# Expert weights in 1 MB loads: two adjacent rows to a partition, in a decoder with two mixture-of-experts layers on one Trainium2 core

## The chip, the core and the metric

The kernel runs on one core of one Trainium2 chip. The time is the device time of one execution in microseconds; three executions of the kernel before took 2774.13, 2776.43 and 2777.44 us.

## What is computed

One sequence of 1024 tokens, 1024 features wide, in float32, passes two layers. The first mixes tokens with a gated DeltaNet, the second with differential attention; each mixer is followed by a layer norm and a hierarchical mixture of experts:

```python
group_prob = softmax(x @ w_group)                 # 4 groups, the best one is taken
in_group = (x @ w_expert) of that group           # 8 experts in it, the best two are taken
hcat = x_rows @ w13[e]                            # [rows, 1024] @ [1024, 1024]
hid = silu(hcat[:, :512]) * hcat[:, 512:]
y_rows = hid @ w2[e]                              # [rows, 512] @ [512, 1024]
h = layer_norm(ALPHA * h + sum of the two gated y_rows)
```

There are 32 experts in a layer, with 6 MB of float32 weights each (w13 4 MB, w2 2 MB), so 192 MB are read per layer.

## The kernel before

The order of the work is: the DeltaNet (`phase_a`), its output projection with the routing logits, `routing` (sorts the tokens by expert, largest expert first, and writes the index tables xidx and yidx), `experts`, `combine` (gates, residual, layer norm), attention (`phase_b_attention`), its output projection, and again `routing`, `experts` and `combine`.

**Experts.** `plan` (L1500) writes out the order of the work: experts in the order of `ORDER`, which mixes large ones with small ones. The numbers of rows that an expert is built for stand in `CAPS`; they are cut into blocks of at most 128 rows. In the first layer all experts have one block, 16 of them of 64 rows or less. In the second layer sizes are uneven: some experts have two or three blocks, and many have 16 to 64 rows. An expert has 12 pieces of weights, 128 rows of 1024 floats each (512 KB): 8 of w13 (the contraction over the features) and 4 of w2 (the contraction over hid). For each piece PE multiplies the block's transposed X or hid with it. The order of use is that of `seq` (L1530): pieces 0 to 4 of an expert's w13, then the 4 pieces of w2 of the expert before it, then pieces 5 to 7.

A block of more than 64 rows works with split weights: `cut_one` (L1426) has ACT cast a piece to `mh` and DVE compute the rest `ml`, and `mm3` multiplies three times. A block of at most 64 rows ("whole") multiplies the piece `mraw` itself, in float32, with two halves of PE's columns side by side. Casts are issued up to `AHEAD` = 9 pieces before the use (`use`, L1474), into a pool of `NHI` = 6 pairs. PE, ACT and DVE each work in the order in which this code issues (`InOrder`, L202).

**The ring of weights.** `Weights` (L1375) loads the pieces one by one from SyncE's queue (`load_one`, L1415) into a ring of slots of 512 KB: in the first layer 13 slots that exist while the output projection runs (5 in the pool m_kept, 8 in m_raw), and 9 more (m_late) once its memory is free; in the second layer 11 and 9. `load` (L1439) issues a load as soon as the code has passed the point where the slot's old piece is done: for a piece that only large blocks use that is its cast, otherwise PE's last use (`held`, L1391). The 12 pieces of the first expert go into the pool of mh and ml (`load_first`, L1433). The experts 1 and 2 are known before the routing (`FIXED`), and the ring is filled with them as far as it goes (`load_fixed`, L1451); later experts' numbers are read from `eid`.

**Gathers and transposes.** A block's rows of h are gathered by POOL with an indirect DMA into one of four X buffers (L1581), issued two experts ahead (`gather`, L1701). `trx` (L1607) transposes X with PE, 128 columns at a time, `trh` (L1646) does so with hid; the matrix to be transposed is PE's stationary operand, so a transpose has a weight load of that data and a matmul with the identity. Results are scattered to y in DRAM by POOL (L1671).

**Combine.** `combine` (L1785) loads y, two rows per token, 1 MB at a time (`yin`, L1802: rows 2p and 2p+1 of 256 to partition p), adds it to h and normalizes. h, and ln_ffn_g and ln_ffn_b, use slots of the weights' pools (`tile` and `spare`); in the first layer so do the first weights of the attention (`start`, L946).

Names in the profile: `mraw` is a weight piece in the ring (in combine also h, g or b), `mh` and `ml` the split piece, `xT`/`hT` and `xTw`/`hTw` the transposed operands of large and whole blocks, `mtr` and `mtw` the PSUM tiles of transposes, `acc` the products, `in_w` the weights in DRAM. L210 is the helper of `InOrder`, so all instructions of PE, ACT and DVE in the experts have this line; L1423 is the weight load.

Of the kernel before, what the change touches and what calls it, by code (L numbers as in the profile page):

```python
# [19 lines left out]
P = 128  # L20
# [22 lines left out]
NRAW, NKEPT, NLATE, NHI, AHEAD = (13, 11), 5, 9, 6, 9  # L43
# [110 lines left out]
def moe_setup(c, es):  # L154

    nc = c.nc
    p = es.enter_context(c.tc.tile_pool(reuse_waits="tile", name="moe", bufs=1, side="right"))
    consts(c, "moe", p)
    c.cb = p.tile([P, 2 * P + 3], BF16, name="cb")
    nc.vector.tensor_copy(c.cb[:, 0:P], c.tris)  # L160
    nc.vector.tensor_copy(c.cb[:, P:2 * P], c.ones)
    nc.vector.tensor_copy(c.cb[:, 2 * P:2 * P + 2], c.colv)
    nc.vector.memset(c.cb[:, 2 * P + 2:], 2.0 * T / P)
    c.tris_b, c.ones_b, c.colv_b, c.none_b = (c.cb[:, a:b] for a, b in ((0, P), (P, 2 * P), (2 * P, 2 * P + 2), (2 * P + 2, 2 * P + 3)))
    c.lg8 = p.tile([P, NT, 8], F32, name="lg8")
# [3 lines left out]
    c.xidx = p.tile([P, 256], I32, name="xidx")  # L169
    c.yidx = p.tile([P, 256], I32, name="yidx")  # L170
    c.ovl = p.tile([1, 2, NCOL + 1], I32, name="ovl")
    c.eid = p.tile([1, NE], I32, name="eid")
# [1201 lines left out]

class Weights:  # L1375
# [5 lines left out]
    def __init__(self, c, layer, kept, raw, seq):  # L1381
        self.late = None
        self.nearly = NRAW[layer]
        self.c, self.seq = c, seq
        self.w13, self.w2 = c.ins["w13"][layer], c.ins["w2"][layer]
        self.kept, self.raw, self.nraw = kept, raw, NRAW[layer] + NLATE
        self.first = [p for p, (r, _) in enumerate(seq) if r == seq[0][0]]
        self.ring = [p for p, (r, _) in enumerate(seq) if r != seq[0][0]]
        self.loaded = self.split = self.free = self.spares = 0
# [6 lines left out]
        self.extra = NKEPT - 2 - (3 if layer == 0 else 0)  # L1396
        self.tiles, self.ids = {}, {}
# [8 lines left out]
    def tile(self):  # L1406

        return self.kept.tile([P, D], F32, name="mraw")

    def spare(self):  # L1410

        self.spares += 1
        return self.tile() if self.spares <= self.extra else self.raw.tile([P, D], F32, name="mraw")

    def load_one(self, eid, i, raw=None):  # L1415
        if raw is None:
            n = self.loaded % self.nraw
            raw = self.tile() if n < NKEPT else (self.raw if n < self.nearly else self.late).tile([P, D], F32, name="mraw")
        if i < KT:
            src = self.w13[bass.ds(eid, 1), i * P:(i + 1) * P]  # L1420
        else:
            src = self.w2[bass.ds(eid, 1), (i - KT) * P:(i - KT + 1) * P]
        self.c.nc.sync.dma_start(raw, src.rearrange("a p f -> (a p) f"))  # L1423
        return raw
# [14 lines left out]
    def load(self, upto):  # L1439
        while self.loaded < min(upto, len(self.ring)):  # L1440
            if self.late is None and self.loaded >= self.nearly:
                return
            if self.loaded >= self.nraw:
                before = self.ring[self.loaded - self.nraw]
                if before >= (self.free if self.held[before] else self.split):
                    return
            r, i = self.seq[self.ring[self.loaded]]
            self.tiles[r, i] = (self.load_one(self.expert(r), i),)
            self.loaded += 1

    def load_fixed(self):  # L1451
        n = 0
        while n < len(self.ring) and self.seq[self.ring[n]][0] < FIXED:
            n += 1
# [84 lines left out]
def weights_open(c, layer, es):  # L1539

    moe_setup(c, es)
    kept = es.enter_context(c.tc.tile_pool(reuse_waits="tile", name="m_kept", bufs=NKEPT, side="right"))
    c.raw2 = ExitStack()
    raw = c.raw2.enter_context(c.tc.tile_pool(reuse_waits="tile", name="m_raw", bufs=NRAW[layer] - NKEPT, side="right"))
    c.jobs, c.steps, seq = plan(layer)
    c.w = Weights(c, layer, kept, raw, seq)


def experts_open(c, es):
# [3 lines left out]
    for x in c.X:  # L1553
        c.nc.gpsimd.memset(x, 0.0)
    c.w.hi = es.enter_context(tc.tile_pool(reuse_waits="tile", name="m_hi", bufs=NHI))
    c.w.late = es.enter_context(tc.tile_pool(reuse_waits="tile", name="m_late", bufs=NLATE))
# [4 lines left out]
def experts(c, layer, h_dram, y_dram):  # L1561
# [4 lines left out]
    with ExitStack() as es:  # L1566
# [22 lines left out]
        def turn(b, src, n, dst):  # L1589
# [3 lines left out]
            for i in range(n):  # L1593
                pe.transpose(pt[:, i, 0:R], src[0:R, i * P:(i + 1) * P], c.ident[0:R, 0:R])
# [4 lines left out]
        def plain(b, src, n, dst):  # L1599
# [3 lines left out]
            for i in range(n):  # L1603
                pe.transpose(pt[:, i, 0:R], src[0:R, i * P:(i + 1) * P], c.ident[0:R, 0:R])
# [140 lines left out]
        c.h = [w.spare() for t in range(HA[layer][1])]  # L1745
# [39 lines left out]
def combine(c, layer, h_dram, y_dram, dst, hT=None):  # L1785

    nc, tc, ins = c.nc, c.tc, c.ins
    with ExitStack() as es:
# [4 lines left out]
        c.h += [c.w.spare() for t in range(HA[layer][1], NT)]  # L1793
# [129 lines left out]
```

## Time and profile before

| | |
|---|---|
| median of three executions | 2776.43 us |
| the profiled execution | 2769.66 us, its span 2767.9 us |
| PE busy in the span | 2420.6 us (87%) |
| DVE, ACT, POOL | 1504.0, 1216.1, 550.2 us |
| moved by DMA | 564.01 MB, mean 204 GB/s; read from HBM 515.58 MB |
| weight loads of the ring | 720 of 512 KB, on SyncE's queue (q1) |
| mean granted PE clock | 0.946 |

The profile is one execution. Its page gives each engine's busy time, the span in 40 slices with the share of busy DMA engines and the rate, the waits with the instruction that ended each, and the DMA queues. Queue q1 is SyncE's, q0 holds POOL's gathers and scatters, q10 is ACT's. A DMA share is the mean over 16 engines of the time that packets took; packets in flight overlap, so it can pass 1. Busy PE is modelled from pipelined matmuls and is not PE at its peak.

### The profile page before, as it was taken

Reading aid. Unit: us, or ns where it says so; the run is one execution under the profiler, and the core shown is the slowest. Engines: PE = TensorE matmul, PEld = TensorE weight load, DVE = VectorE, ACT = ScalarE, POOL = GpSimd, SP = SyncE. Lnnn points to the kernel's source line nnn. Section 1 sums busy time; section 2 is a strip of 40 time slices with the busy share of each in tenths; the row PEclk is TensorE's granted clock in tenths of the full one; section 3 lists DMA queues with packets and bytes.
Section 4 is the critical chain, followed back from the end, with each engine's and each line's share of the span. In section 5 each row is a group of like instructions: output and inputs, shape, how many; then the busy total and the mean of one; then the engine's idle time right before and its main releaser. Section 6 shows DMA issues by size and latency. Waiting matters only on the chain. (4 is left out here: it accounts for less than half of the span.)

```text
span 2767.9 us, 38789 instructions
## 1 busy us (share of the span) xinstructions
PE 2420.6 (87%) x13789; PEld 1646.7 (59%) x13789; DVE 1504.0 (54%) x2696; ACT 1216.1 (44%) x2173; POOL 550.2 (20%) x445
## 2 busy tenths in 40 slices
PE   8999999999969998888559999998987897989990
PEld 5777777777735544444257777776764462545550
DVE  4555555564547554555376766676446432233467
ACT  5455555543425444444245555555332322122454
POOL 3333333331202111010132111111021111011104
PEclk9999999999989999999769999999997998999995
DMA  4121111124779999999831111012537969699885
GB/s 144 50 58 50 58 55 58 47 83 131 249 247 366 391 387 382 382 379 397 336 132 44 33 39 33 31 30 97 198 113 251 404 242 392 242 401 367 309 317 225
DMA packets 195480, 564.01 MB, mean 204 GB/s; under 512 B 40401, under 2 KB 63185, under 8 KB 193233
## 3 DMA queue, kind: packets, MB, share of 16 engines
q1 hardware_dynamic: 178240, 515.07, 50.7%
q0 software_dynamic: 15168, 43.01, 4.5%
q10 hardware_dynamic: 1872, 3.40, 0.4%
q8 instruction: 110, 1.80, 0.3%
q14 instruction: 90, 0.73, 0.1%
HBM read 515.58 MB, written 52.89 MB: 205 GB/s over the span
## 5 line engine op out<-in xcount | busy, mean ns | idle before, releaser
L210 DVE TENSOR_TENSOR ml<-mraw,mh 128x1024 fp32r<-128x1024 f32 x300 | 357.1, 1222 | 269.3 <-ACT mh L210 248.6
L210 ACT CAST mh<-mraw 128x1024 fp32r<-128x1024 f32 x300 | 307.2, 1052 | 272.7 <-DMA mraw<-in_w 205.4
L210 PE MATMUL acc<-mh,xT 128*128 128x512 f32 (+5 forms) x976 | 329.2, 406 | 3.2 <-ACT mh L210 3.2
L210 PE MATMUL acc<-mraw,xTw 128*64 128x512 f32 x1184 | 286.1, 615 | 13.6 <-DVE xTw L210 13.1
L185 POOL TENSOR_TENSOR wl<-raw,wh 128x512 fp32r<-128x512 f32 x106 | 155.1, 1484 | 485.7 <-ACT wh L184 421.4
L210 PEld LDWEIGHTS acc<-mh,xT 128*128 128x128 f32 (+5 forms) x976 | 166.5, 171 | 91.5 <-issue 24.6
L223 PE MATMUL pj<-xh,wh 128*128 128x512 f32 x512 | 217.9, 426 | 0.0
L224 PE MATMUL pj<-xl,wh 128*128 128x512 f32 x512 | 209.3, 409 | 0.0
L1581 POOL DMA_INDIRECT X<-h,xidx x69 | 71.4, 1035 | 689.3 <-PE mtw L210 374.9
L225 PE MATMUL pj<-xh,wl 128*128 128x512 f32 x512 | 207.7, 406 | 0.1
L210 PE MATMUL acc<-ml,xT 128*128 128x512 f32 (+5 forms) x496 | 195.9, 399 | 1.7 <-DVE ml L210 1.7
L223 PE MATMUL pj<-hT,wh 128*128 128x512 f32 (+1 forms) x432 | 165.8, 384 | 8.9 <-DVE kll L1010 5.4
L224 PE MATMUL pj<-hT,wh 128*128 128x512 f32 (+1 forms) x432 | 168.1, 389 | 0.0
L210 PEld LDWEIGHTS acc<-mraw,xTw 128*64 128x64 f32 x1184 | 76.2, 138 | 148.1 <-issue 108.9
L225 PE MATMUL pj<-hT,wl 128*128 128x512 f32 (+1 forms) x432 | 162.3, 376 | 1.7 <-POOL wl L185 1.6
L210 PE MATMUL acc<-mraw,hTw 128*64 128x512 f32 x592 | 143.5, 627 | 19.9 <-ACT hTw L210 19.4
L210 PE MATMUL acc<-mh,hT 128*128 128x512 f32 (+5 forms) x480 | 159.5, 403 | 0.6 <-ACT hT L210 0.5
L408 DVE SCALAR_TENSOR_TENSOR cv<-pr,cw,cv 128x512 f32<-128x512 f32 x144 | 118.9, 826 | 50.9 <-ACT cv L405 48.8
L1114 ACT ACTIVATE e<-sc,sm 128x256 f32<-128x256 f32 (+7 forms) x128 | 94.6, 742 | 89.8 <-DVE sm L1112 89.4
L210 PEld LDWEIGHTS acc<-mh,hT 128*128 128x128 f32 (+5 forms) x480 | 83.0, 173 | 49.7 <-issue 16.2
L225 PEld LDWEIGHTS pj<-xh,wl 128*128 128x128 f32 x512 | 97.2, 190 | 19.9 <-POOL wl L185 0.7
L224 PEld LDWEIGHTS pj<-xl,wh 128*128 128x128 f32 x512 | 97.5, 190 | 18.2 <-issue 1.7
(407 smaller groups left out, 4918.8 us busy)
## 6 DMA issues: line engine op xcount, KB each, us to landing
mraw<-in_w SPq DMA_DIRECT2D x720, 512.0 KB
raw<-in_w_in SPq DMA_DIRECT2D x32, 512.0 KB
yin<-y SPq DMA_DIRECT2D x16, 1024.0 KB
raw<-in_w_kvq SPq DMA_DIRECT2D x21, 512.0 KB
h<-res SPq DMA_DIRECT2D x16, 512.0 KB
p<-ores POOLq DMA_DIRECT2D x12, 512.0 KB, 3.8
res<-p SPq DMA_DIRECT2D x12, 512.0 KB
mh<-in_w SPq DMA_DIRECT2D x12, 512.0 KB
```

Source lines behind the costliest of these rows:

```text
L185: c.nc.gpsimd.tensor_tensor(l[:, s], src[:, s], h[:, s].bitcast(F32), OP.subtract)
L210: out = getattr(self.engine, name)(*args, **kwargs)
L223: mm(out, ah, bh, start=first, stop=False)
L224: mm(out, ah, bl, start=False, stop=False)
L225: mm(out, al, bh, start=False, stop=last)
L408: nc.vector.scalar_tensor_tensor(a, pr[:, 1 + j:513 + j], cw[:, idx, j:j + 1], a, op0=OP.mult, op1=OP.add)
L1114: nc.scalar.activation(e[:, 0:L], st[m][:, 0:L], AF.Exp, bias=sm[:, 2 + m:3 + m], scale=SC, accum_out=sm[:, 4 + m:5 + m])
L1581: c.last_gather = instruction(nc.gpsimd.indirect_dma_start(out=b.X[0:rows], out_offset=None, in_=h_dram, in_offset=bass.IndirectOffsetOnAx ...
```

## The change

A slot of the ring becomes 1 MB, two pieces. One DMA loads 256 rows of w13 or w2: rows 2p and 2p+1 go to partition p, side by side, so each partition gets 8 KB that are contiguous in DRAM. Piece i of a pair now holds rows i%2, i%2+2, ... of the 256, and the transposes of X and hid take every other column to match (`rows_of`). The ring has 7 + 4 slots of 1 MB in the first layer in place of 13 + 9 of 512 KB, and 5 + 5 in place of 11 + 9 in the second. A slot is reused when both of its pieces are done. The pool m_kept is gone; other users take half a slot each, from m_raw. The first expert's pieces are still loaded one by one (128 rows with a row step of two). The index tables are allocated later, beside the X buffers.

```diff
-NRAW, NKEPT, NLATE, NHI, AHEAD = (13, 11), 5, 9, 6, 9
+NRAW, NLATE, NHI, AHEAD = (7, 5), (4, 5), 6, 9
...
+def rows_of(i):
+    return slice(2 * P * (i // 2) + i % 2, 2 * P * (i // 2) + 2 * P, 2)
...
-        self.kept, self.raw, self.nraw = kept, raw, NRAW[layer] + NLATE
+        self.raw, self.nraw = raw, NRAW[layer] + NLATE[layer]
...
-        self.ring = [p for p, (r, _) in enumerate(seq) if r != seq[0][0]]
+        self.ring = [(r, i // 2) for r, i in seq if r != seq[0][0] and i % 2 == 0]
+        self.at = {key: p for p, key in enumerate(seq)}
...
     def tile(self):
-        return self.kept.tile([P, D], F32, name="mraw")
-    def spare(self):
-        self.spares += 1
-        return self.tile() if self.spares <= self.extra else self.raw.tile([P, D], F32, name="mraw")
+        if self.spare is None:
+            t = self.raw.tile([P, 2, D], F32, name="mraw")
+            self.spare = t[:, 1]
+            return t[:, 0]
+        t, self.spare = self.spare, None
+        return t
...
+    def load_one(self, eid, i, raw):
+        w, i = (self.w13, i) if i < KT else (self.w2, i - KT)
+        self.c.nc.sync.dma_start(raw, w[bass.ds(eid, 1), rows_of(i)].rearrange("a p f -> (a p) f"))
         return raw
+    def load_two(self, eid, u, raw):
+        w, u = (self.w13, u) if u < KT // 2 else (self.w2, u - KT // 2)
+        src = w[bass.ds(eid, 1), 2 * P * u:2 * P * (u + 1)]
+        self.c.nc.sync.dma_start(raw, src.rearrange("e (p a) f -> (e p) a f", a=2))
...
             if self.loaded >= self.nraw:
-                before = self.ring[self.loaded - self.nraw]
+                r, u = self.ring[self.loaded - self.nraw]
+                before = self.at[r, 2 * u + 1]
                 if before >= (self.free if self.held[before] else self.split):
                     return
-            r, i = self.seq[self.ring[self.loaded]]
-            self.tiles[r, i] = (self.load_one(self.expert(r), i),)
+            r, u = self.ring[self.loaded]
+            raw = (self.raw if self.loaded % self.nraw < self.nearly else self.late).tile([P, 2, D], F32, name="mraw")
+            self.load_two(self.expert(r), u, raw)
+            for a in range(2):
+                self.tiles[r, 2 * u + a] = (raw[:, a],)
             self.loaded += 1
...
-                pe.transpose(pt[:, i, 0:R], src[0:R, i * P:(i + 1) * P], c.ident[0:R, 0:R])
+                pe.transpose(pt[:, i, 0:R], src[0:R, rows_of(i)], c.ident[0:R, 0:R])
...
-                    pe.transpose(pt[:, k], b.X[0:64, k * P:(k + 1) * P], c.ident[0:64, 0:64])
+                    pe.transpose(pt[:, k], b.X[0:64, rows_of(k)], c.ident[0:64, 0:64])
...
-                    pe.transpose(pt[:, i], b.hid[:, i * P:(i + 1) * P], c.ident)
+                    pe.transpose(pt[:, i], b.hid[:, rows_of(i)], c.ident)
```

## Rows read from the trace of the kernel before

**Rows 1.** the page's slices: the span in 40 parts, busy tenths, GB/s
```profile
DMA  4121111124779999999831111012537969699885
GB/s 144 50 58 50 58 55 58 47 83 131 249 247 366 391 387 382 382 379 397 336 132 44 33 39 33 31 30 97 198 113 251 404 242 392 242 401 367 309 317 225
```

**Rows 2.** windows: stretch, its length, engines' busy us, granted clock, DMA share, GB/s
```profile
845.00:1306.00 461.00, 417.56 (x1901) 224.67 (x1902) 251.71 (x270) 207.70 (x268) 56.64 (x52) 0.97 1.02 385
2106.00:2700.00 594.00, 551.47 (x2544) 300.52 (x2544) 229.25 (x271) 189.75 (x262) 78.25 (x73) 0.96 0.85 323
2145.00:2220.00 75.00, 65.73 (x314) 33.81 (x312) 32.02 (x37) 27.30 (x39) 12.74 (x11) 0.94 1.03 404
2285.00:2348.00 63.00, 49.73 (x240) 17.23 (x236) 13.91 (x19) 11.92 (x21) 9.21 (x8) 0.92 1.03 399
2412.00:2455.00 43.00, 34.54 (x173) 12.30 (x170) 12.12 (x15) 10.10 (x16) 7.30 (x7) 0.95 1.03 404
```

**Rows 3.** waits of PE and of ACT, 845 to 1306: us, times, longest
```profile
PE acc L210 <- ACT hTw L210: 18.9, 9, 3.0
ACT mh L210 <- DMA mraw<-in_w: 152.5, 73, 7.9
```

**Rows 4.** waits of SyncE's queue, 845 to 1345, then 2106 to 2700
```profile
SPq L1423 <- DMA mraw<-in_w: 279.3, 301, 2.8
...
SPq L1423 <- PE acc L210: 189.2, 124, 23.1
```

**Rows 5.** the timeline of ACT: start, us, the group of instructions
```profile
1304.92 1.05 ACT L210 CAST mh<-mraw 128x1024 fp32r<-128x1024 f32 x1 [0.26 <-DVE xTw L210]
```

**Rows 6.** DMA packets: 2090 to 2100; 1359 to 1365; 2719 to 2737
```profile
DMA packets 1130, 4.12 MB, mean 412 GB/s; under 512 B 124, under 2 KB 124, under 8 KB 1130
q1 hardware_dynamic: 1130, 4.12, 103.0%
...
DMA packets 399, 2.46 MB, mean 410 GB/s; under 512 B 36, under 2 KB 36, under 8 KB 162
q1 hardware_dynamic: 399, 2.46, 97.9%
...
DMA packets 1371, 7.55 MB, mean 420 GB/s; under 512 B 145, under 2 KB 145, under 8 KB 753
q1 hardware_dynamic: 1371, 7.55, 101.2%
```

**Rows 7.** DMA packets of 850 to 1300
```profile
DMA packets 48707, 172.80 MB, mean 384 GB/s; under 512 B 6588, under 2 KB 6588, under 8 KB 48674
q1 hardware_dynamic: 43730, 159.24, 92.6%
q0 software_dynamic: 4944, 13.18, 9.0%
```

**Rows 8.** DMA issues, 850:1300, 2350:2400, 777:794; last number us to landing
```profile
X<-h,xidx POOLq DMA_INDIRECT x25, 7.4
...
X<-h,xidx POOLq DMA_INDIRECT x2, 4.9
...
X<-h,xidx POOLq DMA_INDIRECT x4, 10.6
```

**Rows 9.** the timeline of PE at the first layer's start; idle time in brackets
```profile
797.56 1.51 PE L210 MATMUL mtf<-ct_all,X 96*128 96x96 f32 x8 [6.03 <-DMA X<-h,xidx]
```

**Rows 10.** the transposes: ns min, median, max, first and last start; timeline row
```profile
L210 PEld LDWEIGHTS mtw<-ct_all,X x304: 134/139/226, 850.4 to 2654.8; 64*128 64x128 f32 x152
L210 PEld LDWEIGHTS mtw<-ct_all,hidw x76: 138/141/226, 874.4 to 2678.5; 128*128 128x128 f32 x76
...
L210 PEld LDWEIGHTS mtr<-ct_all,X x240: 137/141/231, 808.7 to 2671.3; 128*128 128x128 f32 x48, 96*128 96x128 f32 x24, 80*128 80x128 f32 x20, 112*128 112x128 f32 x12
L210 PEld LDWEIGHTS mtr<-ct_all,hid x120: 137/141/144, 841.3 to 2691.1; 128*128 128x128 f32 x48, 96*128 96x128 f32 x24, 80*128 80x128 f32 x20, 112*128 112x128 f32 x12
...
1328.48 0.71 PE L210 MATMUL mtw<-ct_all,X 64*128 64x64 f32 x8
```

More of the change, by code (lines that the diff above doesn't have):

```diff
@@ L168, in moe_setup @@
     c.gates = p.tile([P, NT, 2], F32, name="gates")
[L169 to L172, printed above, removed]
 def split(c, h, l, src):
@@ L1371, in routing, with __init__ @@
     c.rs.close()
+def rows_of(i):
+    return slice(2 * P * (i // 2) + i % 2, 2 * P * (i // 2) + 2 * P, 2)
 class Weights:
-    def __init__(self, c, layer, kept, raw, seq):
+    def __init__(self, c, layer, raw, seq):
         self.late = None
@@ L1385, in __init__ @@
         self.w13, self.w2 = c.ins["w13"][layer], c.ins["w2"][layer]
-        self.kept, self.raw, self.nraw = kept, raw, NRAW[layer] + NLATE
+        self.raw, self.nraw = raw, NRAW[layer] + NLATE[layer]
         self.first = [p for p, (r, _) in enumerate(seq) if r == seq[0][0]]
-        self.ring = [p for p, (r, _) in enumerate(seq) if r != seq[0][0]]
-        self.loaded = self.split = self.free = self.spares = 0
+        self.ring = [(r, i // 2) for r, i in seq if r != seq[0][0] and i % 2 == 0]
+        self.at = {key: p for p, key in enumerate(seq)}
+        self.loaded = self.split = self.free = 0
+        self.spare = None
         self.cut_rows = [any(m > 64 for m in blocks_of(layer, r)) and r not in NATIVE[layer] for r, _ in seq]
@@ L1395, in __init__ @@
             self.cuts.append(self.cuts[-1] + cut)
-        self.extra = NKEPT - 2 - (3 if layer == 0 else 0)
         self.tiles, self.ids = {}, {}
@@ L1406, in tile @@
     def tile(self):
-        return self.kept.tile([P, D], F32, name="mraw")
-    def spare(self):
-        self.spares += 1
-        return self.tile() if self.spares <= self.extra else self.raw.tile([P, D], F32, name="mraw")
[L1415 to L1423, printed above, removed]
-        return raw
+        if self.spare is None:
[7 more added lines that the diff above has]
+        self.c.nc.sync.dma_start(raw, w[bass.ds(eid, 1), rows_of(i)].rearrange("a p f -> (a p) f"))
+        return raw
+    def load_two(self, eid, u, raw):
+        w, u = (self.w13, u) if u < KT // 2 else (self.w2, u - KT // 2)
+        src = w[bass.ds(eid, 1), 2 * P * u:2 * P * (u + 1)]
+        self.c.nc.sync.dma_start(raw, src.rearrange("e (p a) f -> (e p) a f", a=2))
     def cut_one(self, raw):
@@ L1452, in load_fixed @@
         n = 0
-        while n < len(self.ring) and self.seq[self.ring[n]][0] < FIXED:
+        while n < len(self.ring) and self.ring[n][0] < FIXED:
             n += 1
@@ L1541, in weights_open @@
     moe_setup(c, es)
-    kept = es.enter_context(c.tc.tile_pool(reuse_waits="tile", name="m_kept", bufs=NKEPT, side="right"))
     c.raw2 = ExitStack()
-    raw = c.raw2.enter_context(c.tc.tile_pool(reuse_waits="tile", name="m_raw", bufs=NRAW[layer] - NKEPT, side="right"))
+    raw = c.raw2.enter_context(c.tc.tile_pool(reuse_waits="tile", name="m_raw", bufs=NRAW[layer], side="right"))
+    c.layer = layer
     c.jobs, c.steps, seq = plan(layer)
-    c.w = Weights(c, layer, kept, raw, seq)
+    c.w = Weights(c, layer, raw, seq)
 def experts_open(c, es):
@@ L1554, in experts_open @@
         c.nc.gpsimd.memset(x, 0.0)
+    c.xidx = xp.tile([P, 256], I32, name="xidx")
+    c.yidx = xp.tile([P, 256], I32, name="yidx")
+    c.ovl = xp.tile([1, 2, NCOL + 1], I32, name="ovl")
+    c.eid = xp.tile([1, NE], I32, name="eid")
     c.w.hi = es.enter_context(tc.tile_pool(reuse_waits="tile", name="m_hi", bufs=NHI))
-    c.w.late = es.enter_context(tc.tile_pool(reuse_waits="tile", name="m_late", bufs=NLATE))
+    c.w.late = es.enter_context(tc.tile_pool(reuse_waits="tile", name="m_late", bufs=NLATE[c.layer]))
     c.w.load_first()
@@ L1603, in plain @@
             for i in range(n):
-                pe.transpose(pt[:, i, 0:R], src[0:R, i * P:(i + 1) * P], c.ident[0:R, 0:R])
+                pe.transpose(pt[:, i, 0:R], src[0:R, rows_of(i)], c.ident[0:R, 0:R])
             act_.copy(dst, pt[:, :, 0:R])
@@ L1742, in experts @@
                     act(b)
-        c.h = [w.spare() for t in range(HA[layer][1])]
+        c.h = [w.tile() for t in range(HA[layer][1])]
         n0, n1 = HA[layer]
@@ L1792, in combine @@
         lg, lb = c.w.tile(), c.w.tile()
-        c.h += [c.w.spare() for t in range(HA[layer][1], NT)]
+        c.h += [c.w.tile() for t in range(HA[layer][1], NT)]
         yv = y_dram.rearrange("(t p k) f -> t p k f", p=P, k=2)
```

## Prediction

> **What bounds the kernel now.** I read the page's slices first, then the windows of the two expert stages, then who waits for whom, then the packets. The slices show where the 16 DMA engines are full: nearly all of the first layer's expert stage and most of the second's [rows 1]. In the first layer's stage from 845 to 1306 us the DMA share is 1.02 throughout, at 385 GB/s, while PE is busy 417.6 of 461 us; the 43 us in which PE idles have to be explained [rows 2]. PE's own waits name ACT's copy of hT first, and not a DMA [rows 3]. But ACT works in program order, and its casts of weight rows wait 152.5 us in 73 waits for a weight's DMA; what stands behind such a cast comes late too [rows 3]. So the weights' transfers set the pace, through ACT's and DVE's in-order queues. SyncE agrees: in that stage its weight loads wait almost only for earlier weight loads [rows 4]. After the last cast at 1304.9 us ACT has no cast left to wait for, and PE runs its last experts without such a wait; that tail belongs to PE [rows 5].
>
> In the second layer PE is busy 551.5 of 594 us. Its idle time sits in three places, each at the end of a stretch with full DMA engines: 2145 to 2220, 2285 to 2348 and 2412 to 2455 us, with 9.3, 13.3 and 8.5 us of idle PE [rows 2]. Elsewhere the ring is full: SyncE's loads wait 189.2 us for PE to give a slot back [rows 4]. So what counts here is how much the loads can win within those three stretches.
>
> **The change, part by part.**
>
> *Longer rows.* A load of one 512 KB piece writes one row of 4 KB to each partition; the new one writes 8 KB, contiguous in DRAM and in the partition. No weight moves in this way before, but yin does, 1 MB at a time. The 10 us from 2090 hold weights alone: 103.0% of 16 engines for 10 us are 164.8 engine-us, for 1006 packets of 4 KB (4.12 MB) and 124 small ones [rows 6]. The six us from 1359 hold yin and some 4 KB rows: 0.979 x 16 x 6 = 94.0 engine-us for 36 small, 126 of 4 KB and 237 of 8 KB; the 18 us from 2719 give 291.5 for 145, 608 and 618 [rows 6]. With a small packet at 0, a 4 KB packet costs 0.164 us and an 8 KB packet 0.310 in both windows; with a small one at 0.05 us, 0.158 and 0.305 in both. Per MB on one engine: 16 packets and 2 small ones, 2.62 us, against 8 and 1, 2.48 or 2.49 us: some 5.2% less. But full engines show a share of 1.03 with 4 KB packets and 1.01 with 8 KB, which takes up to 1.8% of it back: 3.5 to 5.2%. Weights hold 92.6 of some 102 points of the first layer's share [rows 7], so such a stretch shortens by 3.2 to 4.7%; I take 4.0%. Bounds: nothing, if what yin shows doesn't hold beside gathers and scatters, and 4.7%.
>
> First layer: 461 us x 4.0% = 18.4 us (0 to 21.7). It fits into PE's 43 us of idle time, so PE does not become the bound. Second layer: 75 + 63 + 43 = 181 us x 4.0% = 7.2 us (0 to 8.5), below the 31 us of idle time at their ends. The start (800 to 845, ring full) and the tail after the last cast gain nothing.
>
> *Two rows share a slot.* The memory is the same (22 pieces become 11 slots in the first layer, 20 become 10 in the second), but a slot comes free with its second row, so a load starts up to one piece later: between 0 and 512 KB at 412 GB/s = 1.27 us, 0.6 in the middle. And the first row of a pair is usable only when both have landed: again 0 to 1.27 us, 0.6. While the engines are full neither adds up, since the order of bytes is all that shifts. It counts once at each place where a full ring turns into full engines and at the cast that ends the wait: 1.3 us in the first layer, 3 x 1.3 = 3.9 us in the second. In the order of use the previous expert's w2 pieces stand between w13's pieces 4 and 5; now piece 5 comes before them and holds a half slot longer, which is inside these bounds.
>
> *Gathers.* A gather shares the engines with the weights. Its landing takes 4.9 us where the engines are part idle, 7.4 in the full stage, and 10.6 at the first layer's start [rows 8]. There PE waits for it, 6.0 us [rows 9]. The Trainium skill (DMA: Bandwidth & Descriptors, Queues, rings and completion order) says that an engine changes between its queues only at the end of a packet, a bundle of descriptors, which speaks against this change: bundles of rows twice as long keep a gather waiting twice as long. By this rule the first layer would lose 2.5 us where PE waits for its first gather, and nothing if packet length did not matter; no run here shows which. From the rows alone the bounds of the cost at the first layer's start are 0 and the whole excess 10.6 - 4.9 = 5.7 us; I take 2, near the excess of the full stage, 7.4 - 4.9 = 2.5. Later gathers go out two experts ahead on POOL's queue, not SyncE's, so those two experts' work covers them. Without that cover each would cost such an excess, 2.5 us. In the second layer PE begins with no such wait.
>
> *Transposes of every other column.* X and hid are the stationary operand, so the step is in a weight load of 128 columns: 139 to 141 ns each, 740 of them in these four rows [rows 10]. None with a step is in this trace. Bounds: nothing, and once more 0.14 us x 740 = 104 us, taken as half in each layer. I take nothing: eight transposes stand in 0.71 us, less than their eight loads one by one, so the loads run beside other work [rows 10]. The Trainium skill (SBUF — State Buffer, Door 1) says that two accesses in one 16-byte line keep full bandwidth; a step of two floats does just that. By this rule the cost is nothing, by the outer bound up to 104 us of PE.
>
> *The rest costs nothing.* SyncE issues half as many loads, and it isn't late now (it waits 0.93 us a load [rows 4]). The first expert's 12 loads stay single, with the row step doubled; they are 4 KB packets as before. h, ln_ffn_g, ln_ffn_b and phase B's first weights take halves of slots that the last experts free long before the scatters end; if they did not, the combine would start a piece later, 1.3 us. The index tiles only move in memory.
>
> **The sum.** First layer -18.4 + 1.3 + 2 = -15.1; second -7.2 + 3.9 = -3.3, of which I keep -2 because a shorter stretch also meets PE sooner. Together -17 us. The profiled execution took 2769.7 us (its span is 2767.9), so 2753; the median of the runs shown, 2776.4, lies 6.8 us higher, which gives 2759 us.
>
> **The rivals.**
> - *The rate stays.* The 8 KB rows of yin win only in quiet windows; in the expert stage, with 9% of the share in gathers and scatters, the weights stay at 385 GB/s. For: the stage already runs below the 412 of the quiet window. Against: both yin windows agree. Then only the costs are left: 1.3 + 2 + 3.9 = 7 us at most, 0 if they hide: 2776 to 2784. Chance 0.13.
> - *Pairs eat most of it.* Both halves of the slot's cost stand at their bounds in the second layer's three places (2 x 1.27 in place of 1.3 us), the half slots held over w2 cost another piece there (1.27), and the first gather pays 5.7: -17 + 3 x 2.5 + 3.7, about -6: 2770. For: SyncE waits long for slots there [rows 4]. Against: while the engines are full, no bytes are lost. Chance 0.13.
> - *Slower: strided weight loads.* Each transpose takes 0.14 us more. In the first layer 52 us use up all 43 us of idle PE, so that stage gains nothing and loses 9; in the second PE is 93% busy [rows 2], so some 48 us come through: 9 - 2 + 48 = +55, 2831 us. It decides from 17 / (370 x 0.93) = 0.05 us per transpose on. For: no weight load with a step is in the trace. Against: the same elements are loaded, and most loads run beside matmuls. Chance 0.09, with smaller such losses.
>
> **How the numbers follow.** The forecast (-10 to -31) has 0.65. About 0.2%, 5.5 us, is what a measurement of this kernel can tell. Faster by more: 0.65 and half of the second rival, 0.72. Within: its other half and half of the first, 0.13. Slower: the other half of the first and the third, 0.15. The range runs from -31 (21.7 + 8.5, no costs) to +7 (no rate, all costs): 2745 to 2784.
>
> **What would show it.** Right: the 461 us stretch is some 18 us shorter, at about 400 GB/s; weight packets of 8 KB; ACT's waits on the weights' DMA shrink in total, fewer and longer; PE's idle time falls to about 25 us. Wrong: the same GB/s with 8 KB packets (first rival); second-layer stalls over 31 us (second); transposes' weight loads well over 0.14 us (third). A PE that is busy throughout with engines no longer full would mean that I took the wrong bound.

## The result and the profile after: 0.7% slower

The changed kernel took 2794.89 us (median of four runs, 2794.26 to 2797.67) against 2776.93 us of the kernel before timed beside it: ratio 1.0067, 95% interval 1.005 to 1.0085. The prediction, 2759 us and faster, was wrong in sign. The profiled execution took 2797.67 us, its span is 2795.8 us. The medians below are of executions in the faster state: one of the six of e4_pairs_of_512kb took 4050.18 us and the other five 2791.29 to 2795.94, so its median is 2791.81 us, and not the 2793.78 that expectations written after it start from.

The slices of the page after (busy tenths of the DMA engines, GB/s), to be held against [rows 1]:

```profile
DMA  4111111124769999999721111003627959698685
GB/s 150 42 57 57 50 54 57 58 87 147 250 235 378 400 383 398 379 397 413 272 87 39 33 32 40 30 30 113 232 93 264 407 211 401 231 378 356 254 350 223
```

The engines are full in the same places. In the first layer the rate is up (378 to 413 where it was 366 to 397). The windows of the two expert stages (columns as in [rows 2]):

```profile
845.00:1302.00 457.00, 424.26 (x1910) 237.80 (x1910) 249.80 (x271) 205.83 (x269) 65.49 (x52) 0.99 1.00 391
2110.00:2700.00 590.00, 543.92 (x2428) 303.79 (x2428) 212.99 (x251) 175.62 (x243) 75.14 (x70) 0.95 0.81 318
```

The DMA packets of 850 to 1300 and the landing of the gathers issued then, against [rows 7, 8]:

```profile
DMA packets 27444, 177.23 MB, mean 394 GB/s; under 512 B 4219, under 2 KB 4219, under 8 KB 7434
q1 hardware_dynamic: 22474, 163.72, 91.6%
...
X<-h,xidx POOLq DMA_INDIRECT x25, 8.1
```

So the longer rows act as forecast, in the first layer: 22474 packets in place of 43730 move 2.8% more, 394 GB/s in place of 384, while the share of the full engines goes from 1.02 to 1.00. But PE takes 424.3 of 457 us and idles for 33, not for 25. Who waited for whom, ACT and then SyncE in the first stage (845 to 1302 and 845 to 1345), then SyncE in the second (2110 to 2727):

```profile
ACT mh L206 <- DMA mraw<-in_w: 128.3, 34, 10.8
...
SPq L1427 <- PE acc L206: 196.7, 63, 8.9
SPq L1427 <- DMA mraw<-in_w: 103.5, 61, 3.5
SPq L1427 <- DVE ml L206: 86.7, 43, 7.3
...
SPq L1427 <- PE acc L206: 352.7, 95, 15.4
```

Against [rows 3, 4]: ACT's waits for weights did shrink, 152.5 to 128.3 us, fewer and longer, as forecast. SyncE's waits changed their kind. Before, its loads in the first layer waited for earlier loads (279.3 us); now mostly for a slot (196.7 + 86.7 us). In the second layer the wait for PE to give a slot back went from 189.2 to 352.7 us. The ring, not the engines, holds the loads back more often. At last the transposes, against [rows 10]:

```profile
L206 PEld LDWEIGHTS mtw<-ct_all,X x304: 191/213/220, 851.5 to 2684.2; 64*128 64x128 f32 x152
L206 PEld LDWEIGHTS mtw<-ct_all,hidw x76: 195/196/219, 875.7 to 2707.9; 128*128 128x128 f32 x76
...
L206 PEld LDWEIGHTS mtr<-ct_all,X x240: 194/216/231, 809.3 to 2700.6; 128*128 128x128 f32 x48, 96*128 96x128 f32 x24, 80*128 80x128 f32 x20, 112*128 112x128 f32 x12
...
2205.25 1.17 PE L206 MATMUL mtw<-ct_all,X 64*128 64x64 f32 x8
```

A weight load with a step of two takes 196 to 216 ns in place of 139 to 141, and eight transposes of a whole block 1.17 us in place of 0.71.

### The profile page after: what moved, and what is told of

Read it like the earlier page. It is cut to its first block, busy times and chain, and to the rows that moved or that the text cites. A ratio compares the mean times of both kernels' runs of the same rounds, so it can differ in the third digit from the quotient of the medians.

```text
span 2795.8 us, 37175 instructions
## 1 busy us (share of the span) xinstructions
PE 2448.3 (88%) x13789; PEld 1682.1 (60%) x13789; DVE 1501.8 (54%) x2696; ACT 1212.2 (43%) x2173; POOL 557.5 (20%) x445
## 5 line engine op out<-in xcount | busy, mean ns | idle before, releaser
L206 PE MATMUL acc<-mraw,xTw 128*64 128x512 f32 x1184 | 288.1, 619 | 24.9 <-DVE xTw L206 24.8
L220 PEld LDWEIGHTS pj<-xl,wh 128*128 128x128 f32 x512 | 97.3, 190 | 17.9 <-issue 1.4
## 6 DMA issues: line engine op xcount, KB each, us to landing
mraw<-in_w SPq DMA_DIRECT2D x360, 1024.0 KB, 15.8
```

What stands on the lines that cost most here:

```text
L206: out = getattr(self.engine, name)(*args, **kwargs)
L220: mm(out, ah, bl, start=False, stop=False)
```

## The experiments

Each kernel was timed together with the kernel before on the same chip, whose median was 2775.3 us beside e1 to e4, 2775.39 beside e5 to e8 and 2775.94 beside e9 to e12. The stages are read from PE's timeline of each kernel's one profiled execution: the first layer from the first transpose of X to the last product, from there to combine's first transpose, in the second layer from the start of the routing's run of seven counts (`pc<-M,cb`) to the first transpose of X, and from there to the last product.

| kernel | median us | ratio, interval | layer 1 stage | to combine | layer 2 start | layer 2 stage |
|---|---|---|---|---|---|---|
| before | 2775.3 | | 551.1 | 25.5 | 18.1 | 591.5 |
| after | 2794.89 | 1.0067, 1.005 to 1.0085 | 546.5 | 28.1 | 21.7 | 612.8 |
| e1 after, no step in the transposes | 2788.04 | 1.0044, 1.0029 to 1.006 | 543.5 | 28.1 | 21.7 | 602.5 |
| e2 before, with the step | 2792.11 | 1.0056, 1.004 to 1.0071 | 558.7 | 25.6 | 18.0 | 606.6 |
| e3 1 MB loads, 4 KB rows, no step | 2794.05 | 1.0066, 1.0049 to 1.0083 | 552.8 | 28.0 | 21.3 | 608.8 |
| e4 pairs of two 512 KB loads, no step | 2791.81 | 1.006, 1.0042 to 1.0078 | 555.4 | 27.9 | 21.3 | 605.6 |
| e5 = e4, w2 between pairs | 2789.35 | 1.0047, 1.0031 to 1.0063 | 554.8 | 28.9 | 21.3 | 598.8 |
| e6 = e4, tables in place | 2789.71 | 1.0053, 1.0038 to 1.0068 | 557.2 | 27.4 | 18.1 | 601.8 |
| e7 before, w2 as in e5 | 2778.01 | 1.0008, 0.9997 to 1.0018 | 556.0 | 25.3 | 18.1 | 596.3 |
| e8 before, two slots fewer | 2794.25 | 1.0063, 1.0045 to 1.0081 | 557.6 | 26.8 | 18.0 | 608.8 |
| e9 after, no step for whole blocks' X | 2788.49 | 1.0043, 1.0029 to 1.0056 | 546.4 | 28.2 | 22.6 | 608.2 |
| e10 = e1 with e5's and e6's repairs | 2779.44 | 1.0006, 0.9997 to 1.0015 | 543.4 | 27.8 | 18.8 | 604.8 |
| e11 pairs in layer 1 only, no step | 2774.09 | 0.9992, 0.9982 to 1.0003 | 545.5 | 27.9 | 18.1 | 594.9 |
| e12 = e11 with the step | 2774.48 | 0.9992, 0.9981 to 1.0002 | 547.2 | 28.1 | 17.9 | 599.4 |

One caution for the stages: e11 and e12 run the second layer with the slots, order and loads of the kernel before, and their one profiled execution shows 594.9 and 599.4 where that of before shows 591.5. A profiled execution can also lie up to 7 us from its kernel's median: that of before, 2769.7 us, lies 6 us under it, that of e1 (2781.33) 7 under, that of e12 (2780.60) 6 above. A few us between single profiles say nothing; the medians carry the verdicts, the profiles say where.

### First group: which part costs

The theories were P, the pairs cost, and S, the step costs. Four kernels take the change apart.

**e1_plain_turns.** The weights are loaded as in the change, and the transposes take contiguous columns, so they read other columns of X and hid than the rows of the weights ask for.

```diff
-                pe.transpose(pt[:, i, 0:R], src[0:R, rows_of(i)], c.ident[0:R, 0:R])
+                pe.transpose(pt[:, i, 0:R], src[0:R, i * P:(i + 1) * P], c.ident[0:R, 0:R])
```

(and so in the other three places)

PE runs 13789 instructions in the profile of every kernel here, so the other values that e1, e9 and e10 compute don't change the amount of its work.

> The changed kernel with its 1 MB loads of 8 KB rows, but the transposes of X and hid read contiguous columns again (so the products pair columns with other rows of the weights; the amount of work is the same). Theory S, strided weight loads: in the changed kernel eight transposes of X take 1.17 us in place of 0.71, and the 740 loads 196 to 216 ns in place of 139 to 141; taking the step away should give back about 17 us in the second layer, where PE is the bound, and uncover in the first layer the gain of the longer rows (10 us or more): 2763 to 2778 us. Theory P, the paired slots (the ring waits for PE 353 us in place of 189 in the second layer): the step was hidden, so at most 5 us come back: 2788 to 2795 us.

**e2_strided_turns.** The kernel before, with `rows_of` as in the change in its single loads and in its transposes:

```diff
-            src = self.w13[bass.ds(eid, 1), i * P:(i + 1) * P]
+            src = self.w13[bass.ds(eid, 1), rows_of(i)]
```

> The kernel before with its 512 KB loads and single slots, but each piece takes every other row of 256 (4 KB rows as before) and the transposes take every other column: the step alone. Theory S: 15 to 25 us slower than before, 2792 to 2802 us, most of it in the second layer. Theory P: within 4 us of before, 2773 to 2781 us.

**e3_1mb_4kb_rows.** The changed kernel, whose 1 MB load puts rows p and 128 + p into partition p; no step anywhere:

```diff
-    return slice(2 * P * (i // 2) + i % 2, 2 * P * (i // 2) + 2 * P, 2)
+    return slice(i * P, (i + 1) * P)
-        self.c.nc.sync.dma_start(raw, src.rearrange("e (p a) f -> (e p) a f", a=2))
+        self.c.nc.sync.dma_start(raw, src.rearrange("e (a p) f -> (e p) a f", a=2))
```

> The changed kernel with 1 MB loads and paired slots, but rows p and 128 + p go to partition p: 4 KB rows, and contiguous columns in the transposes. Against the run with plain transposes and 8 KB rows it tells the row's length apart: by my prediction's first step 8 KB rows win some 15 us in the first layer's expert stage, so this run should take 10 to 20 us more than that one; if the row's length is worth nothing, the two agree within 4 us. Theory S together with the first step: 2775 to 2790 us. Theory P: 2788 to 2800 us.

**e4_pairs_of_512kb.** `rows_of` as in e3, and a slot's two halves loaded by two DMAs of 512 KB:

```diff
-        src = w[bass.ds(eid, 1), 2 * P * u:2 * P * (u + 1)]
-        self.c.nc.sync.dma_start(raw, src.rearrange("e (p a) f -> (e p) a f", a=2))
+        for a in range(2):
+            src = w[bass.ds(eid, 1), rows_of(2 * u + a)]
+            self.c.nc.sync.dma_start(raw[:, a], src.rearrange("a p f -> (a p) f"))
```

> Paired slots alone: each slot of 1 MB is filled by two loads of 512 KB with 4 KB rows, contiguous columns in the transposes. Theory P: the whole loss is here, 10 to 20 us slower than before, 2787 to 2797 us. Theory S: the pairs cost what I took for them, 1.3 us in the first layer and 4 in the second, so 2777 to 2783 us.

What follows: neither theory alone. e1, e3 and e4 came out as theory P has it, e2 as theory S has it. The pairs alone cost 16.5 us (e4 less before). One DMA of 1 MB in place of two makes no difference that can be told: e3's median is 2.2 us above e4's, and their intervals overlap; so it isn't seen to matter either that both halves become usable together. The 8 KB rows win 6.0 us (e1 less e3; all six executions of e1 lie below all six of e3). The step costs 5 to 7 us on top: 6.9 by the medians of after and e1, 5.2 when each is held against the kernel before timed beside it (18.0 and 12.7), and the two intervals overlap. These four lead from before to after by construction, each being the step from one kernel to the next. Put on the kernel before alone, the step comes with a loss of 16.8 us. (e2 has the step in its loads' rows too, and its first layer runs at 379 GB/s from 850 to 1300 in place of 384; how much of the 16.8 that is was not tried.)

The rate of e3 and of e1, packets of 850 to 1300:

```profile
DMA packets 46828, 174.92 MB, mean 389 GB/s; under 512 B 4184, under 2 KB 4184, under 8 KB 46802
```

```profile
DMA packets 27564, 177.98 MB, mean 396 GB/s; under 512 B 4238, under 2 KB 4238, under 8 KB 7472
```

389 against 396 GB/s, with the same pairs and no step in either, is what the 8 KB rows are worth there, beside gathers and scatters. Weights alone, in 8 KB rows, stand in the three us from 2105 in after:

```profile
DMA packets 184, 1.27 MB, mean 423 GB/s; under 512 B 29, under 2 KB 29, under 8 KB 29
```

Against the 412 GB/s of weights alone in 4 KB rows [rows 6] these are 2.7% more.

### Second group: what it is about the pairs

The progress of the second layer (the start of each expert's Silu on ACT's timeline, us from one to the next) shows that e4 loses most of its time in a few places, each at the end of a run of small experts:

| from expert to expert (rank) | before | e4 | e5 | e6 | e8 |
|---|---|---|---|---|---|
| 29 to 8 | 16.0 | 21.2 | 16.0 | 18.8 | 20.8 |
| 19 to 18 | 23.1 | 25.7 | 23.0 | 25.3 | 28.9 |
| 16 to 15 | 16.0 | 22.6 | 18.5 | 22.8 | 20.8 |

Elsewhere e4 and before differ by at most 1.4 us, but for 28 to 27, right behind the first place, where e4 is 2.8 us shorter. e11 and e12, whose second layer is the same code, differ by 1.9 and 3.2 us at the last two places, so e4's 2.6 us from 19 to 18 say little by themselves, while e8 loses 4.8, 5.8 and 4.8 us at the three. At these places PE uses up the ring's pieces faster than the engines refill it. The windows of the last two places, of before, of e4 and of e8 (columns as in [rows 2]):

```profile
2435.75:2458.85 23.10, 14.64 (x67) 5.79 (x64) 9.92 (x11) 8.60 (x12) 3.75 (x3) 0.85 1.03 403
2517.25:2533.25 16.00, 13.39 (x67) 4.87 (x64) 9.76 (x11) 8.41 (x13) 3.34 (x3) 1.00 1.03 398
```

```profile
2452.32:2478.02 25.70, 15.40 (x67) 5.46 (x63) 9.92 (x11) 8.60 (x12) 2.98 (x3) 0.80 1.03 404
2536.52:2559.12 22.60, 15.55 (x67) 5.83 (x64) 9.69 (x11) 8.54 (x13) 2.99 (x3) 0.85 1.03 398
```

```profile
2450.60:2479.50 28.90, 16.66 (x67) 5.56 (x63) 9.91 (x11) 8.55 (x12) 2.98 (x3) 0.76 1.03 405
2538.00:2558.80 20.80, 15.06 (x67) 5.82 (x64) 9.77 (x11) 8.51 (x13) 3.80 (x3) 0.84 1.03 396
```

The same 67 matmuls stand in each window, the engines are full in each, and PE idles (length less busy) 8.5, 10.3 and 12.2 us in the first place, 2.6, 7.1 and 5.7 in the second. But PE's busy time rises as well, from 14.6 to 15.4 and 16.7 and from 13.4 to 15.6 and 15.1 us, with the granted clock lower: 0.85, 0.80, 0.76, and 1.00, 0.85, 0.84. The clock has two levels, 1.2 and 2.4 GHz; a mean below 1.00 is a stretch with some of both. In the first of e8's places it falls while PE waits: the granted clock is 1.00 up to 2462.3 us, PE stands idle for 11.55 us before 2473.91, and from 2465.9 to 2479.4 the clock is 0.50, which is 1.2 GHz. Two groups of eight transposes there, and the two windows:

```profile
2460.26 1.10 PE L210 MATMUL mtr<-ct_all,X 128*128 128x128 f32 x8
2473.91 1.97 PE L210 MATMUL mtr<-ct_all,X 128*128 128x128 f32 x8 [11.55 <-DVE xT L210]
```

```profile
2450.60:2462.30 11.70, 11.01 (x50) 3.14 (x46) 0.42 (x1) 0.71 (x2) 0.00 (x0) 1.00 1.03 397
2465.90:2479.40 13.50, 5.49 (x16) 2.34 (x16) 9.02 (x10) 6.52 (x9) 1.98 (x2) 0.50 1.03 409
```

The same eight transposes take 1.97 us behind the wait and 1.10 before it. So these waits are paid twice, once as idle time and once in slower matmuls after it.

**e5_pairs_w2_between** (on e4) and **e7_single_w2_between** (the same lines on the kernel before):

```diff
-            mid = 4 if n == 1 else 5
+            mid = 4
-            steps += m1[:3] + (tail[0] + m1[3:5] + tail[1] if tail else m1[3:5])
+            steps += m1[:3] + (tail[0] + m1[3:4] + tail[1] + m1[4:5] if tail else m1[3:5])
```

> The paired slots of 512 KB loads again (e4_pairs_of_512kb), but every expert's work order has the previous expert's w2 pieces after w13's piece 3 in place of after piece 4, so no pair is held across w2's four pieces. Counted from the order of the work, the pieces that may be loaded ahead of the one in use are always 20 in the second layer before; with pairs 18.6 on average and 15 at the least; in this order 19.5 and 19. Theory L (pairs cost lookahead: each starvation loses the pieces that are missing when the full ring begins to drain): most of the 14 us of the second layer and of the 4 of the first come back, second layer 594 to 597 us from first transpose to last product in place of 605.6, the whole some 2780 us. Rival G (it is the release of a slot with its second row in general, or the place of the buffers): nothing changes, 2791 to 2796 us.

> The kernel before (single slots) with the work order of e5, w2 after piece 3: the control. Its lookahead is 22 and 20 pieces at every point, as before. Theory L: no change within 0.15%, 2772 to 2779 us. If the order itself is worth something, it shows here, and only what e5 gains beyond it speaks for L.

**e6_tables_in_place** (on e4):

```diff
+    if c.layer == 0:
+        tables(c, xp)
-    c.xidx = xp.tile([P, 256], I32, name="xidx")
...
+    if layer == 1:
+        tables(c, p)
```

> e4_pairs_of_512kb with the index tables of the second layer allocated where they were before, so that the buffers of the first expert's weights lie where they lay and SyncE's queue has their first loads ahead of the last two stores of h again. Theory M (the late start of the second layer, 21.3 us from the routing's last product to the first transpose in place of 18.1, comes from this order): 18 us again, PE's first wait for X about gone, the whole 3 us shorter, 2790 to 2791 us; the stage itself stays at some 604 us. Rival (X is late because of the paired loads): 21 us as in e4, 2794 us.

**e8_two_slots_fewer** (the kernel before):

```diff
-NRAW, NKEPT, NLATE, NHI, AHEAD = (13, 11), 5, 9, 6, 9
+NRAW, NKEPT, NLATE, NHI, AHEAD = (13, 11), 5, 7, 6, 9
```

> The kernel before with 7 late slots in place of 9: 20 pieces of lookahead in the first layer, 18 in the second. Theory L: each of the second layer's three or four starvations loses two pieces of 1.27 us, 8 to 10 us, and the first layer one such, 2.5 us: 2785 to 2788 us. If depth is not what the pairs lose, 2774 to 2778 us.

What follows. Depth is dear here: two slots fewer cost 18.9 us (e8), where theory L had 10 to 13 by the missing bytes alone; the clock comes on top. 15.4 of them stand at the three places, where e4 loses 14.4: the pairs lose time where a shallower ring does. e5 takes the loss out of the first two places and 4 us out of the third, 12.0 us of e4's in all, but its stage is only 6.8 us shorter than e4's: it is 4.3 us longer from 28 to 27 and 1.8 longer from 6 to 14. Its median is 2.5 us below e4's, where theory L expected 14; it lies between what L and G expected, nearer to G's, and the intervals of e4 and e5 overlap. So e5 alone doesn't show that the hold across w2 costs time in the whole; e10 below has it together with e6's edit. The order itself is worth nothing that can be told (e7).

e6's second layer starts after 18.1 us in place of 21.3, as theory M has it; its median, 2789.71 us, is 2.1 below e4's, and these intervals overlap too. The mechanism stands in SyncE's timeline at the second layer's start, of before, then of after, then of e6, each followed by PE's first transpose of X (start, us, idle time in brackets):

```profile
2040.49 22.75 SPq L886 DMA_DIRECT2D h<-res  x3
2071.27 0.33 SPq L1423 DMA_DIRECT2D mh<-in_w  x1
2077.27 0.33 SPq L886 DMA_DIRECT2D h<-res  x1
...
2107.99 1.09 PE L210 MATMUL mtw<-ct_all,X 64*128 64x64 f32 x8
```

```profile
2043.09 40.45 SPq L882 DMA_DIRECT2D h<-res  x5
2083.64 0.39 SPq L1420 DMA_DIRECT2D mh<-in_w  x1
...
2114.72 1.19 PE L206 MATMUL mtw<-ct_all,X 64*128 64x64 f32 x8 [3.67 <-DMA X<-h,xidx]
```

```profile
2049.37 22.74 SPq L891 DMA_DIRECT2D h<-res  x3
2080.13 0.33 SPq L1429 DMA_DIRECT2D mh<-in_w  x1
...
2117.22 1.08 PE L215 MATMUL mtw<-ct_all,X 64*128 64x64 f32 x8
```

The index tables lie in the same pool as the X buffers now, and push the buffers of the first expert's weights (`mh`, `ml`) to other memory, which the output projection gives back later. SyncE's waits of 2040 to 2100 name it, of before, of after and of e6 (us, times, longest):

```profile
SPq L1423 <- PE po L225: 7.9, 1, 7.9
```

```profile
SPq L1420 <- PE pl L894: 3.5, 1, 3.5
```

```profile
SPq L1429 <- PE po L230: 7.9, 1, 7.9
```

The first load waited for the last product of the projection (`po`) before, as it does again in e6, and waits for the last logits (`pl`) now, and in SyncE's order it stands behind all the stores of h: 2083.6 in place of 2071.3 us. POOL issues the first gather 33.9 us after that load before, 24.7 after and 34.3 in e6 (at 2105.2, 2108.3 and 2114.4 us). So the weights still flow when POOL gathers the first X at 2108 us (q1's share of the engines is 98.1% around it, 56.0% before, and 40.3% from 2112.5 to 2117 in e6); the gather lands after 8.9 us in place of 4.7, and PE waits 3.7 us. With the tables where they were, e6 shows no such wait.

The queue's share and the landing of the gathers there (last numbers, % and us), of before, of after, of e6:

```profile
q1 hardware_dynamic: 1050, 3.80, 56.0%
...
X<-h,xidx POOLq DMA_INDIRECT x5, 4.7
```

```profile
q1 hardware_dynamic: 1256, 7.13, 98.1%
...
X<-h,xidx POOLq DMA_INDIRECT x4, 8.9
```

```profile
q1 hardware_dynamic: 210, 0.72, 40.3%
...
X<-h,xidx POOLq DMA_INDIRECT x2, 3.6
```

### Third group: the step, the sum, and a candidate

**e9_whole_X_plain** (on the changed kernel):

```diff
-                    pe.transpose(pt[:, k], b.X[0:64, rows_of(k)], c.ident[0:64, 0:64])
+                    pe.transpose(pt[:, k], b.X[0:64, k * P:(k + 1) * P], c.ident[0:64, 0:64])
```

> The changed kernel with only the X transposes of whole blocks (64 rows) on contiguous columns again; those of larger blocks and of hid keep the step of two. (X's columns then don't match the weights' rows: the transposes' operands are changed, not their number.) Theory W: the step costs 0.46 us for each whole block's eight X transposes, 22 blocks in the second layer, where PE is the bound outside the starvations, 10 us; in the first layer most of 16 x 0.46 hides. So nearly all of the step's 7 us (2794.9 less 2788.0) comes back: 2787 to 2790 us, second layer's stage 10 us shorter than the changed kernel's 612.8. Rival V: the larger blocks' and hid's transposes cost as much: 2791 to 2793 us.

It came out as theory W has it: 2788.49 us, e1's gain within the noise, from this one line (the second layer's stage in the profile is 4.6 us shorter, not 10; single profiles don't settle that). The groups of PE's instructions from 2110 to 2720 us, after and then e9 (count, busy us, mean ns):

```profile
L206 PE MATMUL mtw<-ct_all,X 64*128 64x64 f32 x176 | 25.8, 292 | 3.7 <-DMA X<-h,xidx 3.7
```

```profile
L206 PE MATMUL mtw<-ct_all,X 64*128 64x64 f32 x176 | 16.4, 237 | 4.7 <-DMA X<-h,xidx 4.6
```

9.4 us of PE's busy time for 22 blocks, 0.43 us each. The larger blocks and hid keep their step in e9, with loads as long as before (194 to 216 ns), and e9 is no slower than e1 by the medians. Their transposes are not free of it: all of them together hold PE 42.1 us in e9's second layer and 38.0 in e1's; X with 88 rows takes 277 ns a matmul there in place of 239, with 128 rows 334 in place of 323. These 4 us stay within what the medians can tell.

**e10_pair_costs_undone** has the diffs of e1, e5 and e6 together.

> e1_plain_turns (8 KB rows, pairs, contiguous columns; its X and hid columns don't match the weights' rows) with both repairs: w2 after piece 3 as in e5, and the second layer's tables in place as in e6. Theory: the two causes are separate, so 2788.0 - 4.4 - 4.1 = 2779.5 us, between 2777 and 2782, still not below the kernel before, since half a slot of lookahead (0.5 piece) and the order's own cost stay. Rival: both repairs win the same time in the second layer: 2783 to 2785 us.

Measured 2779.44 us, 8.6 below e1 (9.2 when each is held against its own kernel before), and the intervals lie apart: the two repairs together win time, more than the rival's 2783 to 2785 allows. That the value expected was hit to 0.1 us is luck: 4.4 and 4.1 are counted from 2793.78 us for e4; from 2791.81 they are 2.5 and 2.1, and the same sum is 2783.4 us. The profiles show both at work, in different places: the second layer starts after 18.8 us in place of e1's 21.7, and the three places take 15.8, 24.8 and 20.0 us in place of 17.5, 27.0 and 23.0. (The whole stage, 604.8 us against 602.5, doesn't show it; e1's profiled execution lies 7 us under its median, that of e10 4 above.) How the 8.6 us divide is not shown. With the 8 KB rows' gain the kernel is as fast as before, no faster. Of the pairs' 18.7 us in loads of 1 MB (e3 less before) some 9.5 remain (2779.44 less 2775.94, and the 6.0 that the rows win). Half a piece of lookahead less on average (by e8's 9.4 us for each slot some 5 us), the order's own cost and combine's later start (27.8 us in place of 25.5) are my explanation of these; no run tells them apart, nor from the place of the buffers, which rival G named.

**e11_pairs_first_layer** and **e12_same_with_steps**: a slot has two pieces in the first layer and one in the second (`side_by_side` in e11 alone).

```diff
+NRAW, NLATE, NHI, AHEAD = (7, 11), (4, 9), 6, 9
+TWO = (2, 1)
...
+def side_by_side(w):
+    first = w[0].reshape(NE, -1, 2, P, D).transpose(0, 1, 3, 2, 4)
+    return np.stack([first.reshape(w[0].shape), w[1]])
```

> A candidate that keeps what the change gains and leaves what it costs: pairs with 8 KB rows in the first layer alone, the second layer with single 512 KB slots, tables and work order as before, all transposes on contiguous columns; for that the first layer's expert weights are laid out with the rows of a pair side by side when the inputs are laid out, outside the time (w_in and the attention's weights are rearranged there already). From e1's stages: first layer 543.5 in place of 551.1 us, start of combine up to 2.5 later, second layer as before: 5 to 7 us below the kernel before, 2768 to 2771 us. If the first layer's gain is given back later it stays at 2775.

> The same as e11_pairs_first_layer, but with the weights as they are given and the first layer's transposes with a step of two. The step costs the first layer 3 us (after against e1: 546.5 and 543.5): 2771 to 2774 us, 0 to 0.15% below the kernel before.

Both stand 0.08% below the kernel before, with intervals that reach to 1.0003 and 1.0002: no gain that these runs can tell. e11 lies 3 us above the 2768 to 2771 us expected, e12 half a us above its 2771 to 2774. The first layer's stage is 5.6 us shorter in e11, and 2.4 us of it are given back before combine begins. No version here beats the kernel before.

## Why the prediction was wrong, step by step

**What bounds the kernel: right for the kernel before.** The rate rose where the engines are full, and ACT's waits shrank with it. But the three stretches of the second layer are not the three places where depth decides. From 16 to 15 (2517 to 2533 us of before) PE idled 2.6 us only, and I didn't count it; there e4 loses most, 6.6 us. In the second stretch (23 to 22) it loses 1.4.

***Longer rows*: right in kind, too large, and the largest miss.** I took 4.0%, the runs show 1.8% from e3 to e1 (389 to 396 GB/s) and 2.6% from before to after (384 to 394). Even weights alone, in short windows, run only 2.7% faster (423 against 412 GB/s), so the 3.5 to 5.2% worked out from yin did not hold for weight loads; why it did not was not tried. The lower bound, nothing, was the honest reminder that no expert stage had been seen with 8 KB packets. Of 25.6 us, 6.0 came.

***Two rows share a slot*: the step that failed.** "While the engines are full neither adds up" holds for bytes in flight, but the loss comes in when the engines are *not* full: while a large expert holds PE and the ring stands full, the pairs stop 1.4 pieces earlier on average and up to 5 at worst, and those pieces are missing when the run of small experts drains the ring. I wrote that piece 5 "holds a half slot longer, which is inside these bounds"; in truth the pair (4, 5) blocks the four slots of w2 behind it as well, because slots are given out in turn. 5.2 us were taken, 16.5 (e4) to 18.7 (e3) measured, some 3 of them at the second layer's start, through the tables. I had priced a missing piece at 1.3 us a place, and e8 shows 9.4 us for a slot: at each of the three places 2.4 to 2.9, as the wait and the clock after it. That the pairs cost so much is shown, and that a shallower ring costs time in the same places; how much of it is the hold across w2 is not, and some 9.5 us stay without a test.

***Gathers*: nearly right in the first layer, wrong in the second.** PE's first transpose of the first layer, after and e3:

```profile
798.36 1.53 PE L206 MATMUL mtf<-ct_all,X 96*128 96x96 f32 x8 [7.01 <-DMA X<-h,xidx]
```

```profile
796.88 1.51 PE L206 MATMUL mtf<-ct_all,X 96*128 96x96 f32 x8 [6.04 <-DMA X<-h,xidx]
```

6.6 to 7.3 us in the six kernels with 8 KB rows in the first layer, 5.3 to 6.0 in seven of the eight with 4 KB rows: about 1 us in place of the 2 taken. That goes the way of the rule that I named (the Trainium skill, DMA: Bandwidth & Descriptors, Queues, rings and completion order), at less than half of what I worked out by it. But e8, with 4 KB rows, waits 7.9 us, so these single profiles don't show that the length of the rows is the cause. "In the second layer PE begins with no such wait" became false by a cause that I had put under *The rest costs nothing*: "The index tiles only move in memory." They move the buffers beside them too, and with these the order of SyncE's queue.

***Transposes of every other column*: the second step that failed.** I took nothing, because eight transposes stood in less than eight loads one by one. They follow their loads all the same: with loads of 139 ns the eight take 0.71 us, 89 ns each, with loads of 213 ns 146 each. The rule that I set beside it (the Trainium skill, SBUF — State Buffer, Door 1: two accesses in one 16-byte line keep full bandwidth) does not hold for these weight loads of float32 with a step of two: 139 to 213 ns. That the rows had no load with a step was said; the rival built on it had the right sign and the whole blocks' 0.43 / 8 = 0.054 us per transpose stand just at its threshold of 0.05. Its price (0.14 us for every one of 740) was too high: the whole blocks' X pay nearly all that the medians show, and in the first layer more than half of that hides (16 x 0.43 = 6.9 us, of which the stage of after shows 3.0 over e1's). It cost 5 to 7 us, not 55.

***The rest*, otherwise: nearly right.** Half as many issues of SyncE and one DMA of 1 MB were worth nothing that can be told. Combine's start came 2.6 us later (28.1 after 25.5), above the 1.3 that I named if its cover failed.

The sum, by the medians: pairs in loads of 1 MB +18.7 where I had +5.2, step +5.2 to +6.9 where I had 0, rows -6.0 where I had -25.6; what I took for gathers is in these. Slower had a chance of 0.15, and by the strided loads most of all; the second rival, which named the pairs, stopped at 6 us faster.

## What to carry to other kernels

When a ring's slots are merged, its bytes stay and its depth does not: walk through the order of use and count, at each point, how many pieces may be loaded ahead; the worst point is where a slot is held across other work, and it counts where the ring begins to drain. Price a slot by taking one or two away before changing its grain. A buffer that moves can change the order of a queue, so read the queue's order before and after. And short matmuls with large stationary operands can follow their weight loads, as the transposes of 64 rows do here: look there before the layout of that operand is changed.

## What the runs showed of the hardware that I had not expected

A longer wait cost clock as well: the same 67 matmuls took 14.6 us with 8.5 us of idle time among them at a granted 0.85 and 16.7 us with 12.2 us at 0.76. It also makes equal code differ: the place from expert 16 to 15 took 16.0 us in e11 and 19.2 us in e12, which are the same there, with 2.7 and 3.6 us of idle time, at a granted 1.00 and 0.85:

```profile
2519.08:2535.08 16.00, 13.35 (x67) 4.88 (x64) 9.75 (x11) 8.40 (x13) 3.37 (x3) 1.00 1.03 397
```

```profile
2525.31:2544.51 19.20, 15.60 (x67) 5.76 (x63) 9.69 (x11) 8.36 (x12) 3.15 (x3) 0.85 1.03 396
```

And a DMA of 1 MB was no better than two of 512 KB into the same slot here (2794.05 and 2791.81 us); what won time was the length of the rows (2788.04 us).

A weight load of TensorE took longer with a step of two floats, 139 ns without and 213 with it for 64 rows.
